# Three of four panels of a norm turned in 32x32 blocks on VectorE and moved by DMA, and the last GLA head ordered right behind its values

## The chip, the cores and the metric

The kernel is one launch on one core of a Trainium2 chip. Its time is device time in microseconds (us), and runs of the two kernels are compared on the same chip. The engines are TensorE (PE; the loading of its weights is shown as PEld), VectorE (DVE), ScalarE (ACT), GpSimd (POOL) and SyncE (SP), which here only issues transfers.

## The reference

A decoder trunk of two layers works on one sequence of 256 tokens by 2048 features, with 256 memory tokens. All is float32.

```
for i in range(DEPTH):                        # DEPTH = 2
    if i == 1:
        fk, fv, fc = fox_shared_kv(x, ...)    # rmsnorm(x) @ w_kv, forget gates
    h = rmsnorm(x, norm_mix[i])
    x = x + (gla_mixer if i == 0 else fox_mixer)(h, ...)
    h = rmsnorm(x, norm_ffn[i])
    x = x + conv_ffn(h, ...)                  # 2048 -> 2 x 5632 -> 2048
return rmsnorm(x, norm_final)
```

The first layer mixes with chunked gated linear attention (GLA, 4 heads), the second with forgetting attention (FoX, 12 heads). Both also attend to the memory tokens with 4 more heads, and the output projection takes all of these side by side. The GLA mixer scales each head's output by a norm of its own and multiplies it with a gate, silu(og). A projection contracts over features, so it wants h with features on the partitions; x itself is kept with tokens on the partitions. Between the two x has to be turned.

## The kernel before

**Products.** Every weight is cut into a high part that PE takes in a single pass and a low remainder. `split_unit` (line 189) loads a unit of 128x1024 floats (512 KB) into one of four `raw` buffers (line 200), ScalarE makes `whi` (205) and VectorE `wlo` (206), each with four buffers. Activations are kept as two halves too: `split` (302) lets ScalarE write the high half times the norm's gain (309) and VectorE the remainder (310). A projection with features out, `proj_fm` (209), runs 32 products of 128x512 on the high parts (line 230) and 32 of 128x256 on the low parts (228). A projection with tokens out, `proj_tm` (242), takes per unit 8 products on `whi` and 4 on `wlo` (line 271), for two token blocks of 128.

**Order.** The body is one program text, and a scheduler with a model of the machine puts it in order on each engine before it runs. `high_priority(offset=AHEAD)` draws weight loads and casts forward, and `issue_after` keeps an instruction behind a named one. Each engine then works strictly in its order, and so does SP's queue of transfers, on which all weight loads stand.

**Where x is turned.** `add_out` (862) runs a projection in four panels of 512 features; its `evac` adds a panel to x (865) and calls `then(f, b)` for token block b. `preparing(name, dst, also)` (903) makes that `then`: it adds squares for the norm's sums (393), and once both token blocks of a panel are there it turns the panel: 8 transpositions of 128x128 on PE into PSUM bank `ps_s` (916), and four `split` calls from PSUM into `dst` (918). It is used three times: behind the first output projection for `ffn0`, behind the down projection of the first feed-forward for the FoX keys and values (`kv`), and behind the second output projection for `ffn1`. At `kv` two norms with different gains need the same x: `also` (930) copies the first 12 turned chunks from PSUM into the buffer `vt` (932), which is not yet in use, and `fox` (757) splits them from there for its queries (`stash`, lines 759 and 769). The final norm keeps tokens on partitions and turns nothing.

**Around the last GLA head.** `gla` (532) runs through the heads: gates (579), query, key and value projections, then `core` (602), which prepares decayed copies of queries and keys on VectorE and ScalarE and makes the scores in small products on PE (651, 658, 667, 673: the half tiles between chunks, the levels inside a chunk, and the rest). `core(hd, ..., ahead)` has `issue_after(ends[-1])`, the last product of the value projection, and `issue_after(ahead)`; `ahead` is the product that spreads the norm of the head before (`made[1].spread`, line 377), except for head 0. `outputs` (696) multiplies scores with values (703, 704), and `scale` (712) applies the head's norm, made by `mean` (334) and `row` (375 to 380). Six gate projections `take_og` (717) follow, two of them before the last head's values; the last head's `outputs` is called at `j == OG_EARLY + 1` and its `scale` at `j == OG_EARLY + 2`. The first output projection takes the memory heads' chunks first, then those of the GLA heads in order.

Of the kernel before, what the change touches and what calls it, by code (L numbers as in the profile page):

```python
# [12 lines left out]
F32 = mybir.dt.float32  # L13
F32R = mybir.dt.float32r
I32 = mybir.dt.int32
AF = mybir.ActivationFunctionType
ALU = mybir.AluOpType
PSUM = bass.MemoryType.PSUM

P = 128  # L20
T = 256
# [4 lines left out]
GLA_H, DK, DV = 4, 256, 384  # L26
# [14 lines left out]
OG_EARLY = 2  # L41
# [99 lines left out]
def _trunk(ctx: ExitStack, tc: tile.TileContext, xt, xtok, memt, wp, wgu, gns, gfin, cnv, par, msk, out):  # L141
    nc = tc.nc
    where, _ = _layout()
    V, S, TE = nc.vector, nc.scalar, nc.tensor
# [8 lines left out]
    part = const.tile([P, C_N], F32, name="part")  # L153
# [6 lines left out]
    def gain(name, i):  # L160
        c = C_GAIN[name] + i
        return gains[:, c : c + 1]
# [6 lines left out]
    x = [const.tile([P, 2, 512], F32, name=f"x{f}") for f in range(4)]  # L169
    bufA = [const.tile([P, 2, T], F32R, name=f"A{i}", tag=f"A{i}") for i in range(KC)]  # L170
# [11 lines left out]
    loads, casts, ends = [], [], []  # L182
# [119 lines left out]
    def split(dst, i, src, g=None):  # L302

        hi, lo = dst[i][:, 0, :], dst[i][:, 1, :]
        if g is None:
            S.activation(hi, src, AF.Copy)  # L306
            V.tensor_tensor(lo, src, hi.bitcast(F32), ALU.subtract)
        else:
            S.activation(hi, src, AF.Copy, scale=g)
            V.scalar_tensor_tensor(lo, src, g, hi.bitcast(F32), ALU.mult, ALU.subtract)  # L310

    class Norm:

# [142 lines left out]
    nx = StreamNorm()  # L456
# [75 lines left out]
    def gla(nx):  # L532
        h, mix = bufB, bufA
        with tc.tile_pool(name="gla", bufs=1) as gp:
# [161 lines left out]
            def outputs(hd, v):  # L696
                at = att[hd % 2]
                nrm = Norm(DV, "o" if hd < GLA_H - 1 else "m")
                os = []
                for j in range(3):  # L700
                    po = work("o")
                    vs = slice(j * P, (j + 1) * P)
                    TE.matmul(po[:, :T], v[:, 0, vs], at[:, :T], start=True, stop=False)  # L703
                    TE.matmul(po[:, P:T], v[:, 1, vs], at[:, T:], start=False, stop=True)  # L704
                    o = gp.tile([P, T], F32, name="onorm", tag="onorm", bufs=9)
                    on[3 * hd + j] = o
                    S.activation(o, po[:, :T], AF.Copy)
                    nrm.add(o)
                    os.append(o)
                return hd, nrm, os  # L710

            def scale(hd, nrm, os):
                for j, o in enumerate(os):
                    f = C_GN + 3 * hd + j
                    V.scalar_tensor_tensor(o, o, part[:, f : f + 1], nrm.row(), ALU.mult, ALU.mult)
# [13 lines left out]
            for hd in range(GLA_H):  # L729
                bc = gates(hd)  # L730
                q = gp.tile([P, 2, T], F32, name="gq", tag="gq", bufs=2)
                k = gp.tile([P, 2, T], F32, name="gk", tag="gk", bufs=2)
                v = values(hd) if hd else v0
                proj_fm(("gq", hd), h, lambda c, a: V.scalar_tensor_tensor(
                    q[:, c, :], whole(a), DK ** -0.5, nx.row(), ALU.mult, ALU.mult))
                if hd:
                    made = outputs(hd - 1, vs)
                proj_fm(("gk", hd), h, lambda c, a: V.tensor_tensor(k[:, c, :], whole(a), nx.row(), ALU.mult))
                if hd:
                    scale(*made)  # L740
                if hd == GLA_H - 1:
                    for j in range(OG_EARLY):
                        take_og(j)
                if hd:
                    proj_tm(("gv", hd), h, lambda b, a: S.activation(
                        v[:, b, :], a, AF.Copy, scale=nx.col()[:, b : b + 1]))
                core(hd, q, k, bc, made[1].spread if hd else ends[-1])
                vs = v
            for j in range(OG_EARLY, 6):
                if j == OG_EARLY + 1:  # L750
                    made = outputs(hd, vs)
                if j == OG_EARLY + 2:
                    scale(*made)
                take_og(j)


    def fox(nx, vt):
        hk, hq, mix = bufB, bufA, bufB
        stash = vt.rearrange("p b (i t) -> p (b i) t", t=T)
        with (  # L760
            tc.tile_pool(name="fox", bufs=1) as fp,
            tc.tile_pool(name="foxd", bufs=1, space=bass.MemoryType.DRAM) as dp,
# [3 lines left out]
            for j in range(6):  # L766
                proj_fm(("fk", j), hk, lambda c, a, j=j: V.tensor_tensor(kt[:, 2 * j + c, :], whole(a), nx.row(), ALU.mult))
                for i in range(2 * j, 2 * j + 2):
                    split(hq, i, stash[:, i, :], gain("mix1", i))
            cs = fp.tile([P, T], F32, name="fc")  # L770
            cc = fp.tile([P, 2, FOX_H], F32, name="fcc")
            take, turn = turned(fp, work("s", 2), FOX_H, nx.col())
# [89 lines left out]
    def add_out(key, src, then=None, spare=None, last=None):  # L862
        for f in range(4):
            def evac(b, a, f=f):
                V.tensor_tensor(x[f][:, b, :], x[f][:, b, :], a, ALU.add)
                if then is not None:
                    then(f, b)

            proj_tm((*key, f), src, last if f == 3 and last is not None else evac, spare if f == 3 else None)

    def ffn(l, nx, h, m, then, spare=None, last=None):
        with tc.tile_pool(name=f"ffn{l}", bufs=1) as fp:
            cw = fp.tile([P, 4 * 88], F32, name="cw")
            nc.sync.dma_start(cw, cnv[l])
            us = [fp.tile([P, T + 2], F32, name=f"u{i}") for i in range(4)]
            for u in us:
                nc.gpsimd.memset(u[:, :2], 0.0)
            turn = [0]
            for p, (lo, hi) in enumerate(PARTS):
                for j in range(lo, hi):  # L880
                    cv = {}

                    def evac(c, a, j=j, cv=cv, i=j - lo):
                        u = us[turn[0] % 4]
                        turn[0] += 1
                        V.tensor_tensor(u[:, 2:], whole(a), nx.row(), ALU.mult)  # L886
                        col = (c * 44 + j) * 4
                        w = [cw[:, col + n : col + n + 1] for n in range(4)]
                        r = fp.tile([P, T], F32, name=f"cv{c}", tag=f"cv{c}", bufs=3)
                        S.activation(r, u[:, 2:], AF.Identity, bias=w[3], scale=w[2])  # L890
                        V.scalar_tensor_tensor(r, u[:, 1 : T + 1], w[1], r, ALU.mult, ALU.add)
                        V.scalar_tensor_tensor(r, u[:, :T], w[0], r, ALU.mult, ALU.add)
                        cv[c] = r
                        if c == 1:
                            S.activation(cv[0], cv[0], AF.Silu)
                            V.tensor_tensor(r, cv[0], r, ALU.mult)  # L896
                            split(m, i, r)

                    proj_fm(("up", l, j), h, evac)
                end = p == len(PARTS) - 1  # L900
                add_out(("down", l, p), m, then if end else None, spare if end else None, last if end else None)

    def preparing(name, dst, also=None):
        n = StreamNorm()

        def then(f, b):
            n.add(f, b)
            if b == 0:
                return
            for i in range(4 * f, 4 * f + 4, 2):  # L910
                ps = work("s", 2)
                for j in range(2):
                    for c in range(2):
                        o = j * T + c * P
                        k = (i + j) % 4 * P
                        TE.transpose(ps[:, o : o + P], x[f][:, c, k : k + P], ident)  # L916
                for j in range(2):
                    split(dst, i + j, ps[:, j * T : (j + 1) * T], gain(name, i + j))
                if also is not None:
                    also(i, ps)  # L920

        return n, then

    gla(nx)
    n, then = preparing("ffn0", bufB)
    add_out(("wo", 0), bufA, then)
    with tc.tile_pool(name="stash", bufs=1) as st:
        vt = st.tile([P, 2, FOX_H * HD], F32, name="fvt")

        def also(i, ps):  # L930
            if i < 12:
                S.activation(vt.rearrange("p b t -> p (b t)")[:, i * T : (i + 2) * T], ps, AF.Copy)
            else:
                for j in range(2):
                    split(bufA, i + j, ps[:, j * T : (j + 1) * T], gain("mix1", i + j))

        n2, then = preparing("kv", bufB, also)
        ffn(0, n, bufB, bufA, then)
        fox(n2, vt)
    n, then = preparing("ffn1", bufA)  # L940
    add_out(("wo", 1), bufB, then)


    fin = StreamNorm()
# [115 lines left out]
```

## Time and profile before

| | |
|---|---|
| three runs | 2284.09 to 2286.19 us, median 2285.31 |
| the profiled execution | 2284.91 us, span 2282.9 |
| PE, DVE, ACT busy | 2269.7, 1588.6, 1259.0 us |
| weights loaded by SP's queue | 809 transfers, most of 512 KB |
| L916, transpositions of x on PE | 96 |

The profile shows one execution. A row of a timeline is start, length, engine, line, operation, output<-inputs, shape and count of merged instructions. A group has busy time and the mean length of one instruction in ns. PE's instructions overlap, so lengths and busy times of small ones are more than the time they take up; starts tell that. What is idle on an engine costs nothing unless it lies on the chain that ends last.

### The profile page before, as it was taken

To read this page: it belongs to the slowest core of one execution; us is meant where nothing else is said; L and a number is where in the kernel's file an instruction comes from. 1 tells how busy PE (TensorE), PEld (TensorE's weight loads), DVE (VectorE), ACT (ScalarE), POOL (GpSimd) and SP (SyncE) were. 2 spreads that over 40 slices of the span, in tenths; PEclk is the share of its full clock that TensorE was granted. 3 is DMA by queue.
4 is the path that set the end of the run, shared out by engine and by line. 5 is a ranking of instruction groups with operands and counts; after the bars stand their busy time and mean duration, and the time that the engine had idled before them with its cause. 6 is when DMAs were issued, how large, how long until landed. Compare 5 with 4: busy or idle time off the path is not lost.

```text
span 2282.9 us, 33393 instructions
## 1 busy us (share of the span) xinstructions
PE 2269.7 (99%) x12417; PEld 1985.8 (87%) x12417; DVE 1588.6 (70%) x2618; ACT 1259.0 (55%) x2001; POOL 3.4 (0%) x19
## 2 busy tenths in 40 slices
PE   9999999999999999999999999999999999999998
PEld 8889998788888888888888998888888888888887
DVE  7769786677765777557766567657776577756775
ACT  6656576555553555445565555556554455534554
POOL 0000000000000000000000000000000000000000
PEclk9999999999999999999999999999999999999999
DMA  9655555555566555655555665555666566665664
GB/s 342 195 164 168 177 171 168 165 183 190 190 194 193 185 192 190 199 186 191 190 187 179 183 195 166 174 191 178 194 189 198 186 190 187 194 194 185 193 194 147
DMA packets 125610, 430.19 MB, mean 188 GB/s; under 512 B 14204, under 2 KB 19464, under 8 KB 125320
## 3 DMA queue, kind: packets, MB, share of 16 engines
q1 hardware_dynamic: 124872, 427.27, 58.0%
q8 instruction: 97, 1.59, 0.3%
q10 hardware_dynamic: 576, 0.79, 0.1%
q14 instruction: 65, 0.53, 0.1%
HBM read 425.90 MB, written 2.11 MB: 187 GB/s over the span
## 4 chain that ended last, share of the span: by engine, by line
PE 99%; DVE 0%; ACT 0%; issue 0%; DVEq 0%; ACTq 0%
PE acc L230 39%; PE acc L271 37%; PE acc L228 20%; PE ps_s L916 0%; PE ps_s L658 0%; PE ps_t L409 0%; PE ps_o L430 0%; PE ps_s L430 0%; PE ps_s L828 0%; PE ps_o L844 0%; PE ps_o L703 0%; PE ps_o L180 0%; PE ps_o L845 0%; PE ps_s L827 0%; PE ps_o L704 0%; PE ps_t L377 0%
## 5 line engine op out<-in xcount | busy, mean ns | idle before, releaser
L206 DVE TENSOR_TENSOR wlo<-raw,whi 128x1024 fp32r<-128x1024 f32 (+4 forms) x809 | 969.1, 1201 | 562.6 <-ACT whi L205 463.6
L205 ACT ACTIVATE whi<-raw 128x1024 fp32r<-128x1024 f32 (+4 forms) x809 | 840.2, 1039 | 607.4 <-PE acc L271 324.3
L230 PE MATMUL acc<-B,whi 128*128 128x512 f32 x2112 | 496.5, 390 | 0.0
L230 PEld LDWEIGHTS acc<-B,whi 128*128 128x128 f32 x2112 | 391.1, 188 | 77.6
L271 PE MATMUL acc<-whi,mix 128*128 128x512 f32 x1280 | 321.8, 391 | 2.6 <-ACT mix L306 2.6
L230 PE MATMUL acc<-mix,whi 128*128 128x512 f32 x1248 | 303.5, 391 | 0.0
L271 PEld LDWEIGHTS acc<-whi,mix 128*128 128x128 f32 x1280 | 240.3, 188 | 52.7 <-ACT mix L306 2.8
L228 PEld LDWEIGHTS acc<-B,wlo 128*128 128x128 f32 x2112 | 264.6, 191 | 5.7
L230 PEld LDWEIGHTS acc<-mix,whi 128*128 128x128 f32 x1248 | 230.2, 188 | 45.2
L228 PE MATMUL acc<-B,wlo 128*128 128x256 f32 x2112 | 269.4, 283 | 0.0
L271 PE MATMUL acc<-whi,B 128*128 128x512 f32 (+3 forms) x960 | 218.1, 363 | 0.0
L271 PEld LDWEIGHTS acc<-whi,B 128*128 128x128 f32 x960 | 174.5, 188 | 17.8
L271 PE MATMUL acc<-wlo,mix 128*128 128x512 f32 x640 | 175.9, 392 | 0.0
L228 PEld LDWEIGHTS acc<-mix,wlo 128*128 128x128 f32 x1248 | 157.8, 191 | 4.3
L228 PE MATMUL acc<-mix,wlo 128*128 128x256 f32 x1248 | 161.3, 284 | 0.0
L271 PEld LDWEIGHTS acc<-wlo,mix 128*128 128x128 f32 x640 | 120.1, 189 | 24.7
L230 PE MATMUL acc<-A,whi 128*128 128x512 f32 x544 | 133.7, 390 | 0.0
L237 ACT ACTIVATE part<-acc 128x256 f32<-128x256 f32 x244 | 92.4, 379 | 61.4 <-PE acc L230 61.3
L271 PE MATMUL acc<-wlo,B 128*128 128x512 f32 (+3 forms) x480 | 120.8, 363 | 0.0
L230 PEld LDWEIGHTS acc<-A,whi 128*128 128x128 f32 x544 | 101.6, 188 | 20.7
L306 ACT ACTIVATE mix<-cv 128x256 fp32r<-128x256 f32 x60 | 25.1, 418 | 161.3 <-DVE cv L896 161.3
L890 ACT ACTIVATE cv<-u,cw 128x256 f32<-128x256 f32 x176 | 104.9, 596 | 8.7 <-DVE u L886 8.6
(230 smaller groups left out, 1674.7 us busy)
## 6 DMA issues: line engine op xcount, KB each, us to landing
raw<-wp SPq DMA_DIRECT2D x743, 512.0 KB, 3.7
raw<-wp SPq DMA_DIRECT2D x32, 384.0 KB, 3.4
raw<-wp SPq DMA_DIRECT2D x24, 388.0 KB, 3.5
raw<-wp SPq DMA_DIRECT2D x8, 400.0 KB, 3.3
xf<-xt SPq DMA_DIRECT2D x16, 128.0 KB, 5.5
x<-xtok SPq DMA_DIRECT2D x4, 512.0 KB, 9.0
mt<-memt SPq DMA_DIRECT2D x7, 256.0 KB, 6.5
cb<-cdram SPq DMA_DIRECT2D x12, 128.0 KB, 3.1
```

Of the source, the lines that this page charges most:

```text
L205: casts.append(S.activation(hi[:, s], raw[:, s], AF.Copy))
L206: V.tensor_tensor(lo[:, s], raw[:, s], hi[:, s].bitcast(F32), ALU.subtract)
L228: TE.matmul(acc[c][:, :T], w[:, s], both[:, 0, :], start=False, stop=False)
L230: TE.matmul(acc[c], w[:, s], both, start=u == j == 0, stop=(u, j) == (3, 3))
L237: S.activation(t, a[:, T:], AF.Copy)
L271: mm = TE.matmul(acc[b][:, :n], src[kcs[j] - base][:, part, b * P : (b + 1) * P], w, start=u == 0 and low == part == j == 0, stop=u == end ...
L306: S.activation(hi, src, AF.Copy)
L890: S.activation(r, u[:, 2:], AF.Identity, bias=w[3], scale=w[2])
```

## The change

For panels 0 to 2 of the three turned norms, PE no longer turns x. VectorE turns each 128x512 token block in 32x32 blocks into a buffer `blk`; when both token blocks are done, 16 transfers of 32 partitions by 1 KB put the blocks on their partitions in a second buffer, and `split_turned` makes the halves from there: one pass of 128x256 on ScalarE and two of 128x128 on VectorE for each chunk. Panel 3 stays on PE. At `kv` the second buffer is the `vt` area itself, so the copies from PSUM are gone, and `fox` splits from that area with `split_turned`.

In `gla` the last head's `core` is no longer held behind the spread of the head before, only behind its own value projection (`ends[-1]`), and its `scale` is called together with its `outputs`, one gate earlier.

```diff
+    def split_turned(dst, i, z, name):
+        g = gain(name, i)
+        hi, lo = (dst[i][:, part, :].rearrange("p (b q j) -> p b q j", b=2, q=4) for part in range(2))
+        src = z[:, :, i % 4].rearrange("p q b j -> p b q j")
+        S.activation(hi, src, AF.Copy, scale=g)
+        for b in range(2):
+            V.scalar_tensor_tensor(lo[:, b], src[:, b], g, hi[:, b].bitcast(F32), ALU.mult, ALU.subtract)
...
-                core(hd, q, k, bc, made[1].spread if hd else ends[-1])
+                core(hd, q, k, bc, made[1].spread if 0 < hd < GLA_H - 1 else ends[-1])
...
                 if j == OG_EARLY + 1:
-                    made = outputs(hd, vs)
-                if j == OG_EARLY + 2:
-                    scale(*made)
+                    scale(*outputs(hd, vs))
...
                 for i in range(2 * j, 2 * j + 2):
-                    split(hq, i, stash[:, i, :], gain("mix1", i))
+                    split_turned(hq, i, stash[i // 4], "mix1")
...
+        def turned_panel(f, b):
+            if b == 0:
+                blocks[f] = pool.tile([P, 4, 4, 2, 32], F32, name="blk", tag="blk", bufs=2)
+            y = blocks[f]
+            V.transpose(y[:, :, :, b, :], x[f][:, b, :].rearrange("p (k c i) -> p c k i", c=4, i=32))
+            if b == 0:
+                return
+            z = pool.tile([P, 4, 4, 2, 32], F32, name="turn", tag="turn", bufs=2) if kept is None else kept[f]
+            for q in range(4):
+                for c in range(4):
+                    nc.sync.dma_start(z[32 * c : 32 * (c + 1), q], y[32 * q : 32 * (q + 1), c])
+            for k in range(4):
+                split_turned(dst, 4 * f + k, z, name)
...
         def then(f, b):
             n.add(f, b)
+            if f < 3:
+                turned_panel(f, b)
+                return
             if b == 0:
                 return
...
         def also(i, ps):
-            if i < 12:
-                S.activation(vt.rearrange("p b t -> p (b t)")[:, i * T : (i + 2) * T], ps, AF.Copy)
-            else:
-                for j in range(2):
-                    split(bufA, i + j, ps[:, j * T : (j + 1) * T], gain("mix1", i + j))
+            for j in range(2):
+                split(bufA, i + j, ps[:, j * T : (j + 1) * T], gain("mix1", i + j))
```

More of the change, by code (lines that the diff above doesn't have):

```diff
@@ L750, in gla, with fox @@
                 if j == OG_EARLY + 1:
-                    made = outputs(hd, vs)
-                if j == OG_EARLY + 2:
-                    scale(*made)
+                    scale(*outputs(hd, vs))
                 take_og(j)
-    def fox(nx, vt):
+    def fox(nx, vt, stash):
         hk, hq, mix = bufB, bufA, bufB
-        stash = vt.rearrange("p b (i t) -> p (b i) t", t=T)
         with (
@@ L901, in ffn, with preparing @@
                 add_out(("down", l, p), m, then if end else None, spare if end else None, last if end else None)
-    def preparing(name, dst, also=None):
+    def preparing(name, dst, pool, kept=None, also=None):
         n = StreamNorm()
+        blocks = {}
+        def turned_panel(f, b):
[11 more added lines that the diff above has]
+                split_turned(dst, 4 * f + k, z, name)
         def then(f, b):
             n.add(f, b)
+            if f < 3:
+                turned_panel(f, b)
+                return
             if b == 0:
@@ L924, in _trunk @@
     gla(nx)
-    n, then = preparing("ffn0", bufB)
-    add_out(("wo", 0), bufA, then)
+    with tc.tile_pool(name="turn0", bufs=1) as tp:
+        n, then = preparing("ffn0", bufB, tp)
+        add_out(("wo", 0), bufA, then)
     with tc.tile_pool(name="stash", bufs=1) as st:
         vt = st.tile([P, 2, FOX_H * HD], F32, name="fvt")
+        turned3 = vt.rearrange("p b t -> p (b t)").rearrange("p (f q k b j) -> p f q k b j", f=3, q=4, k=4, b=2)
+        turned3 = [turned3[:, f] for f in range(3)]
         def also(i, ps):
-            if i < 12:
-                S.activation(vt.rearrange("p b t -> p (b t)")[:, i * T : (i + 2) * T], ps, AF.Copy)
-            else:
-                for j in range(2):
-                    split(bufA, i + j, ps[:, j * T : (j + 1) * T], gain("mix1", i + j))
[L937 to L941, printed above, removed]
+            for j in range(2):
+                split(bufA, i + j, ps[:, j * T : (j + 1) * T], gain("mix1", i + j))
+        with tc.tile_pool(name="turn1", bufs=1) as tp:
+            n2, then = preparing("kv", bufB, tp, turned3, also)
+            ffn(0, n, bufB, bufA, then)
+        fox(n2, vt, turned3)
+    with tc.tile_pool(name="turn2", bufs=1) as tp:
+        n, then = preparing("ffn1", bufA, tp)
+        add_out(("wo", 1), bufB, then)
     fin = StreamNorm()
```

## The prediction

> **What bounds the kernel now.** The page is read first: its span, part 1 (engines) and part 4 (the chain of work that ended last).
>
> ```profile
> span 2282.9 us, 33393 instructions
> PE 2269.7 (99%) x12417; PEld 1985.8 (87%) x12417; DVE 1588.6 (70%) x2618; ACT 1259.0 (55%) x2001; POOL 3.4 (0%) x19
> ...
> PE 99%; DVE 0%; ACT 0%; issue 0%; DVEq 0%; ACTq 0%
> ```
>
> TensorE is busy for 99% of the span and is 99% of the chain. A busy PE need not be a full one, so the waits of PE come next, and then the windows of the two later stages that the change touches and of one short stretch (columns: the stretch, its length, busy time and count of each engine, granted clock, DMA share, GB/s).
>
> ```profile
> PE acc L271 <- ACT mix L306: 2.6, 1, 2.6
> PE ps_o L180 <- DVE B L177: 1.4, 1, 1.4
> PE ps_t L377 <- DVE dg L375: 1.1, 1, 1.1
> ```
>
> ```profile
> 1137.00:1205.00 68.00, 68.00 (x314) 56.31 (x313) 46.48 (x64) 43.78 (x85) 0.31 (x1) 1.00 0.60 193
> ...
> 1472.00:1560.00 88.00, 88.00 (x423) 73.73 (x422) 52.01 (x76) 45.47 (x80) 0.20 (x4) 1.00 0.58 193
> ```
>
> ```profile
> 413.40:417.50 4.10, 4.04 (x11) 3.19 (x12) 1.18 (x4) 1.68 (x4) 0.20 (x4) 0.58 0.17 46
> ```
>
> PE waits three times in all. L180 is the start and stays. The other two lie together, in the first output projection, and the stretch behind them ran at a granted clock of 0.58. The stages at 1137 and 1472 us, where x is also turned, have no gap on PE at all. So time can come from two things only: less work on PE, and that one stall. DVE has 21.5 us free in 68.
>
> **Part 1: 72 of the 96 transpositions on PE go** (three panels of four, three norms, eight each). The group, then the timeline of PE about one panel:
>
> ```profile
> L916 PE MATMUL ps_s<-mask,x 128*128 128x128 f32 x96 | 14.3, 272 | 0.0
> ```
>
> ```profile
> 1151.17 1.98 PE L271 MATMUL acc<-whi,mix 128*128 128x512 f32 x8
> 1152.99 1.07 PE L271 MATMUL acc<-wlo,mix 128*128 128x512 f32 x4
> 1153.89 1.53 PE L271 MATMUL acc<-whi,mix 128*128 128x512 f32 x6
> 1155.26 0.38 PE L916 MATMUL ps_s<-mask,x 128*128 128x128 f32 x2
> 1155.39 0.71 PE L271 MATMUL acc<-whi,mix 128*128 128x512 f32 x2
> 1155.94 0.39 PE L271 MATMUL acc<-wlo,mix 128*128 128x512 f32 x1
> 1156.17 0.82 PE L916 MATMUL ps_s<-mask,x 128*128 128x128 f32 x6
> 1156.74 0.94 PE L271 MATMUL acc<-wlo,mix 128*128 128x512 f32 x3
> 1157.52 1.98 PE L271 MATMUL acc<-whi,mix 128*128 128x512 f32 x8
> ```
>
> Durations overlap, so slots are read from starts. Twelve products from 1151.17 to 1153.89: 2.72 us, 0.227 each; that is also one weight unit (8 high, 4 low). From 1153.89 to 1157.52, 3.63 us, lie again twelve products and 8 transpositions: (3.63 - 2.72) / 8 = 0.114 us each. 72 x 0.114 = **8.2 us**. The group's busy time gives 14.3 / 96 = 0.149 and 10.7 us, which I keep as an end of the range.
>
> A sentence apart: the Trainium skill, page "TensorE: Matmul & The Clock Gate", section "Part 4: PE-mode transpose", gives about 275 ns for one transposition inside a kernel; an estimate by that page would be 72 x 0.275 = 19.8 us.
>
> **Part 2: the last GLA head moves forward.** PE's timeline at the stall (the brackets are idle time and its cause):
>
> ```profile
> 408.05 1.07 PE L271 MATMUL acc<-whi,mix 128*128 128x512 f32 x4
> 410.21 0.63 PE L377 MATMUL ps_t<-dg,onesr 128*128 128x256 f32 x2 [1.09 <-DVE dg L375]
> 413.46 2.68 PE L271 MATMUL acc<-whi,mix 128*128 128x512 f32 x6 [2.63 <-ACT mix L306]
> 415.94 1.66 PE L271 MATMUL acc<-wlo,mix 128*128 128x512 f32 x4
> 417.44 1.09 PE L271 MATMUL acc<-whi,mix 128*128 128x512 f32 x4
> ```
>
> The four products at 408.05 give their slots up at 408.96. Until 413.46 only the two L377 run, so 4.2 us are lost (3.9 to 4.5, as the two take 0.63 or almost nothing). The ten products up to 417.44 take 3.98 us for 2.27: 1.7 us more, at the clock of 0.58. Together **5.9 us**. The cause is a late chain: the head's norm row (L334 to L377), then gate and split. Its start was held back:
>
> ```profile
> 321.30 3.83 PE L230 MATMUL acc<-B,whi 128*128 128x512 f32 x16
> ...
> 368.23 1.98 PE L271 MATMUL acc<-whi,A 128*128 128x512 f32 x8
> ```
>
> ```profile
> 332.22 2.18 DVE L644 TENSOR_TENSOR gdd<-gdd,gq 128x384 f32<-128x384 f32 x6
> ...
> 371.19 0.61 PE L651 MATMUL ps_s<-gq,gk 128*128 128x128 f32 x4
> ...
> 402.13 0.61 PE L334 MATMUL ps_t<-mask,ssq 128*128 128x128 f32 x4
> ```
>
> VectorE had the operands ready at 334.4, but PE began the head's scores at 371.19, since they were ordered behind the norm of the head before. The four gate projections behind the value projection run from 321.30 to 368.23; without what is interleaved one is 32 products of 0.227 and 32 half ones of 0.12, 11.1 us. In the built order of the changed kernel the scores stand two gates and twelve products in, 321.3 + 22.2 + 2.7 = 346.2, and the head's outputs and norm follow in the last gate. From the norm's L334 to its L377 stand 55 products of 0.227, 12.5 us, where the chain now needs 410.2 - 402.1 = 8.1; from L377 to the first product that needs the result stand 29, 6.6 us, where it now needs 413.5 - 410.2 = 3.3. Both are covered, so the stall goes. What is late next is the norm of the head before: between its L334 and L377 stand 19 products, 21 half ones and two pairs of the last head's, some 8.0 us, and ScalarE has one more table switch in between, as a Silu stands between logarithm and exponential. I put 0.5 us there (0 to 2).
>
> **Part 3: what replaces the transpositions.** Per panel: 2 block turns on DVE, 16 transfers of 32 KB on SP's queue, and splits from SBUF. Prices by the nearest rows:
>
> ```profile
> L206 DVE TENSOR_TENSOR wlo<-raw,whi 128x1024 fp32r<-128x1024 f32 x743 | 906.3, 1223 | 505.8 <-ACT whi L205 409.5 <-issue 59.1 <-PE acc L228 30.8
> L205 ACT ACTIVATE whi<-raw 128x1024 fp32r<-128x1024 f32 x743 | 784.6, 1056 | 557.1 <-PE acc L271 290.0 <-PE acc L230 163.9 <-ACT whi L205 52.6
> ...
> L865 DVE TENSOR_TENSOR x<-x,acc 128x512 f32<-128x512 f32 x62 | 42.4, 686 | 17.8 <-PE acc L271 17.4
> ...
> L310 DVE SCALAR_TENSOR_TENSOR B<-ps_s,gains,B 128x256 fp32r<-128x256 f32 x32 | 14.7, 478 | 9.4 <-ACT B L309 9.4
> ...
> L309 ACT ACTIVATE mix<-fvt,gains 128x256 fp32r<-128x256 f32 x12 | 5.4, 497 | 0.0
> ...
> L822 DVE SCALAR_TENSOR_TENSOR dm<-cb,fcc,mask 128x128 f32<-128x128 f32 x12 | 4.1, 340 | 0.0
> ```
>
> No row shows a block turn. Between a 128x128 pass (0.34) and a 128x1024 pass (1.22) I take the row of its size, 0.69. DVE: 18 x 0.69 = 12.3 us, and 96 low halves of 0.34 for 48 of 0.478, 9.7 us more: 22 us over nine panels, 2.4 us each, beside 5 us or more of free DVE per panel (21.5 us over the four panels from 1137). ScalarE keeps its 48 high halves at about 0.5 us and loses six copies. Neither engine is on the chain, so this costs nothing; were DVE full, PE would wait for the low halves of weights, 2.4 us a panel.
>
> Transfers (KB each, median us from issue to landing; then SP's own time to issue one, min/median/max ns):
>
> ```profile
> raw<-wp SPq DMA_DIRECT2D x743, 512.0 KB, 3.7
> ...
> xf<-xt SPq DMA_DIRECT2D x16, 128.0 KB, 5.5
> x<-xtok SPq DMA_DIRECT2D x4, 512.0 KB, 9.0
> ...
> out<-x SPq DMA_DIRECT2D x4, 128.0 KB, 2.2
> ```
>
> ```profile
> L200 SPq DMA_DIRECT2D raw<-wp x809: 327/328/680, 0.7 to 2254.6; - x162
> ```
>
> The program lets eight transfers be in flight on SP's queue, each waiting for the one eight ahead. So one takes the larger of its issue, 0.33, and landing / 8: 0.28 to 0.69 for landings of 2.2 to 5.5. I take 3.7 / 8 = 0.46. A panel of the down projection lasts 6 units = 16.3 us and needs 16 + 6 transfers: 10.1 us. An output projection has 8 units = 21.8 us and 16 + 8 transfers: 11.0 us. SP keeps up.
>
> New waits: SP waits for the block turn, with weight loads queued behind it; ScalarE and VectorE wait for all 16 transfers, with weight casts queued behind. Cover: four weight buffers, so a cast may begin when PE leaves a unit and PE needs it three units, 8.2 us, later; less its own 1.06 that is 7.1 us. A load is issued about 10.9 us ahead of its cast and lands in 3.7: some 5 us more. The built order puts a panel's splits two casts behind the unit whose landing frees its last transfers, which is just about when these land. The third panel is needed after the next stage's first 7 us and has 1 to 4 us to spare. I cost all this at nothing; without that cover it is what the rival below costs.
>
> **The sum**, against the profiled execution (span 2282.9, whole time 2284.9): 2284.9 - 8.2 - 5.9 + 0.5 = 2271.3. The shown runs have a median of 2285.3, 0.4 above it; I leave the forecast at **2271.3 us**.
>
> **Rivals.**
> - *Small waits take back part*: splits or casts come 0.5 to 1 us late at each of nine panels. For it: the third panel's margin of 1 to 4 us. Against: the 12 us of cover. Price 4.5 to 9 us, **2278**.
> - *The last head stalls elsewhere*, the 5.9 us staying: **2277**. For it: the head before has 8.0 us for a chain with one more table switch. Against: 12.5 and 6.6 us of cover for the last head.
> - *SP's queue becomes the bound* (the slower side). If a turned transfer holds it for t, a down panel needs 16 t + 6 x 0.33 us of 16.3; it keeps up until t = 0.9, a landing of 7 us. Past it each panel slips, and after the 12 us of cover PE waits. At t = 2.2 (transfers one at a time, landing as the stores) a down panel slips by 21 us and an output panel by 16: (3 x 21 - 12) + 2 x (3 x 16 - 12) = 123 us, **2394**. It ends slower than before from about t = 1.4 (22.4 + 2 - 16.3 = 8.1, three times, less 12 = 12; the output panels 22.4 + 2.6 - 21.8 = 3.2 add nothing). For it: x landed in 9.0 us. Against: that was 512 KB beside the first weight loads.
> - *A transposition holds PE for its own 272 ns*: 72 x 0.272 = 19.6 us, **2259.9**. Against: the starts at 1156.17 and 1156.74, six in 0.57 us. This is where the page named above would land.
>
> The rule that speaks against the change stands apart: the Trainium skill, page "DMA: Bandwidth & Descriptors", section "Bandwidth", says that transfers under 64 KB are dominated by descriptors; no run shown here has such a transfer between partitions, and an estimate by its fixed cost of about 2 us would put one at 2.1 us alone, or 0.26 with eight in flight.
>
> **Numbers.** Forecast 0.60; small waits 0.17; stall elsewhere 0.10; SP's queue 0.10; longer transpositions 0.03. The low end takes the busy-time price: 2271.3 - 2.5, rounded to **2268.5**. The high end takes both middle rivals' prices short of their sum, **2281**. Outside remain SP's queue, the long transpositions and a tail of the middle rivals, some 0.2. A change under 0.2% (4.6 us) is about what cannot be told from none: faster is below 2280.7, slower above 2289.9. Faster 0.81, same 0.09 (tails of the middle rivals, and a weak form of SP's), slower 0.10.
>
> **What would show it.** In the new trace: 24 transpositions; PE without a wait in the first output projection and no stretch at a clock of 0.58; scores of the last head near 346 us; block turns near 0.7 us; turned transfers landing within 4 us; no ScalarE or DVE wait on them over about 5 us; PE gapless at the starts of the up and key projections. Any of the last three missed, with PE gaps behind it, makes the forecast wrong; so does a new wait at L377's successor for the third head.

## The result and the profile after

| | before | after |
|---|---|---|
| median (range) | 2285.07 us (2284.09 to 2286.19, 4 runs) | 2272.56 us (2272.54 to 2272.87, 4 runs) |
| span of the profiled execution | 2282.9 us | 2270.7 us |

The ratio is 0.9946, with a 95% interval of 0.9934 to 0.9958: 12.5 us less. The forecast was 2271.3 us, 13.6 us below the profiled execution of before (2284.9). The page of the changed kernel, span, engines and chain of work:

```profile
span 2270.7 us, 33489 instructions
...
PE 2259.8 (100%) x12345; PEld 1977.1 (87%) x12345; DVE 1603.6 (71%) x2684; ACT 1256.6 (55%) x1996; POOL 3.4 (0%) x19
...
PE 99%; ACT 0%; DMA 0%; issue 0%; DVE 0%; SPq 0%; DVEq 0%
```

PE still sets the time. It has 72 instructions fewer and is busy 9.9 us less. VectorE took on 15.0 us and ScalarE lost 2.4; neither shows in the chain. The waits of PE (total, times, longest, in us), and the window that held the slow stretch before:

```profile
PE ps_o L180 <- DVE B L177: 1.4, 1, 1.4
PE ps_o L712 <- ACT onorm L716: 1.0, 1, 1.0
PE acc L271 <- ACT whi L205: 0.5, 1, 0.5
```

```profile
413.40:417.50 4.10, 4.10 (x20) 3.40 (x19) 1.77 (x2) 1.50 (x2) 0.00 (x0) 1.00 0.82 240
```

Both waits of the first output projection are gone, and in the same 4.1 us PE does 20 instructions at a clock of 1.00 instead of 11 at 0.58. There is one new wait, at L712, an output pair of the last head; the 0.5 us belong to the first unit of the program, at 9 us, and not to the change. The new operations, as groups and as DMA issues (the last number is median us to landing), then SP's own time to issue one (ns, min/median/max):

```profile
L921 DVE STREAM_TRANSPOSE blk<-x 128x512 f32<-128x512 f32 x18 | 12.7, 707 | 0.3
...
L319 DVE SCALAR_TENSOR_TENSOR B<-turn,gains,B 128x128 fp32r<-128x128 f32 x24 | 6.7, 346 | 3.6 <-ACT B L317 3.6
...
L317 ACT ACTIVATE B<-turn,gains 128x256 fp32r<-128x256 f32 x12 | 5.1, 498 | 5.7 <-DMA turn<-blk 5.7
...
L944 PE MATMUL ps_s<-mask,x 128*128 128x128 f32 x24 | 3.6, 272 | 0.0
```

```profile
turn<-blk SPq DMA_DIRECT2D x96, 32.0 KB, 3.6
...
fvt<-blk SPq DMA_DIRECT2D x48, 32.0 KB, 3.3
```

```profile
L927 SPq DMA_DIRECT2D turn<-blk x96: 507/588/1520, 408.1 to 1526.7; - x96
L927 SPq DMA_DIRECT2D fvt<-blk x48: 507/588/1335, 1147.4 to 1191.4; - x48
```

Block turns (0.707 us), low halves (0.346), high halves (0.498) and landings (3.6 and 3.3) are near the forecast's 0.69, 0.34, 0.5 and 3.7. The issue is not: 0.588 us where a weight load's 0.33 had been taken.

### The profile page after: what moved, and what is told of

It is laid out like the page before. It is cut to its first block, busy times and chain, and to the rows that moved or that the text cites. A ratio compares the mean times of both kernels' runs of the same rounds, so it can differ in the third digit from the quotient of the medians.

```text
span 2270.7 us, 33489 instructions
## 1 busy us (share of the span) xinstructions
PE 2259.8 (100%) x12345; PEld 1977.1 (87%) x12345; DVE 1603.6 (71%) x2684; ACT 1256.6 (55%) x1996; POOL 3.4 (0%) x19
## 4 chain that ended last, share of the span: by engine, by line
PE 99%; ACT 0%; DMA 0%; issue 0%; DVE 0%; SPq 0%; DVEq 0%
PE acc L230 39%; PE acc L271 37%; PE acc L228 20%; PE ps_s L667 0%; PE ps_t L418 0%; DMA raw<-wp 0%; PE ps_o L439 0%; PE ps_s L439 0%; PE ps_s L834 0%; PE ps_o L850 0%; PE ps_o L712 0%; ACT whi L205 0%; PE ps_s L833 0%; PE ps_o L851 0%; PE ps_s L944 0%
```

## The experiments

Three theories of where 12.5 us came from, and why it was less than the 13.6 forecast. **A**: the transpositions pay their PE slots in full, and the last head pays its stall less something that comes back in its own region. **B**: the head pays in full, and the panels give something back to small waits. **C**: the head pays nearly everything, and the transpositions were hidden beside other work. "Below before" is always against runs of the kernel before on the same chip (medians 2285.33, 2285.51, 2285.54 and 2285.09 in the four groups of runs).

### Each half of the change alone

The last head alone, on the kernel before:

```diff
-                core(hd, q, k, bc, made[1].spread if hd else ends[-1])
+                core(hd, q, k, bc, made[1].spread if 0 < hd < GLA_H - 1 else ends[-1])
...
-                    made = outputs(hd, vs)
-                if j == OG_EARLY + 2:
-                    scale(*made)
+                    scale(*outputs(hd, vs))
```

> The kernel before with the last head's edit alone (scores not held behind the head before, scale called with the outputs); all 96 transpositions stay on PE. Theory A (the panels pay their PE slots, 0.114 us each, and the head pays the stall of 5.9 us less about 2 us that come back: a 1.0 us wait of PE on ScalarE at the third head's last output pair, and about 0.9 us more for score products mixed with output pairs): about -3.9 us, 2281.2. Theory B (the head pays the whole forecast of 5.4 us, and the panels give some back to small waits): about 2279.7. Theory C (the head pays nearly all and the transpositions hide beside other work): about -12, 2273.

Measured: 2280.91 us, 4.4 below before, ratio 0.9981 (0.9972 to 0.9990).

The three panels alone; the diff is the same one turned round, on the changed kernel:

> The changed kernel with the last head as before: three panels of four go over VectorE and transfers, the stall in the first output projection stays. Theory A: 72 x 0.114 = 8.2 us less than before, 2276.9, and the stall's two waits (about 1.1 and 2.6 us) and the stretch at a lowered clock are there again. Theory B: about 7 us less, 2278. Theory C: about 2284.

Measured: 2277.39 us, 7.9 below before, ratio 0.9965 (0.9953 to 0.9977). The two halves make 12.3 of the 12.5 us, so they add up and C falls: the head alone does not give 12 us. The start of the second feed-forward's first up projection on PE shows it without the scatter between runs, in the kernel before, with the head alone, and in the changed kernel:

```profile
1544.96 1.29 PE L230 MATMUL acc<-mix,whi 128*128 128x512 f32 x5
```

```profile
1541.19 3.79 PE L230 MATMUL acc<-mix,whi 128*128 128x512 f32 x16
```

```profile
1532.87 3.79 PE L230 MATMUL acc<-mix,whi 128*128 128x512 f32 x16
```

The head gives 3.77 us, the 72 transpositions another 8.32: 0.116 us each. In the run with the panels alone the stall is there again, and so is the slow clock (last row: the window of before, now at 0.50):

```profile
413.61 2.93 PE L271 MATMUL acc<-whi,mix 128*128 128x512 f32 x6 [2.63 <-ACT mix L306]
416.33 1.91 PE L271 MATMUL acc<-wlo,mix 128*128 128x512 f32 x4
418.04 1.75 PE L271 MATMUL acc<-whi,mix 128*128 128x512 f32 x4
419.63 1.09 PE L271 MATMUL acc<-wlo,mix 128*128 128x512 f32 x4
...
413.40:417.50 4.10, 3.90 (x9) 3.12 (x10) 1.32 (x4) 1.70 (x4) 0.20 (x4) 0.50 0.16 46
```

The wait is the 2.63 us of before to the hundredth, but 14 products behind it, from 413.61 to 419.63, are slow here, and take 6.02 us for 14 x 0.227 = 3.18; before it was 10. The price of one and the same gap so varied by 1.1 us. The Trainium skill, page "TensorE: Matmul & The Clock Gate", section "Why this matters for your kernels", warns of PE gaps over about 3 us because the clock drops behind them; here gaps of 1.09 and 2.63 us, with only two short products between, were enough.

### How many panels

```diff
-            if f < 3:
+            if f < 2:
```

(and for chunks 8 to 11 at `kv` the copies and splits of the kernel before)

> The changed kernel with two panels of four turned by VectorE and transfers and two on PE (48 transpositions on PE instead of 24). Theory A: 24 x 0.114 = 2.7 us slower than the changed kernel, 2275.3, whatever the third panel's late transfers do. Theory B (the third panel, the one with 1 to 4 us to spare, gives back part of its gain): under 2 us slower, 2274.5 or less. If a transposition held PE for its whole 0.272 us: 6.5 us slower, 2279.

Measured: 2275.27 us, ratio 0.9956 (0.9943 to 0.9968), 10.1 below before. Seen from the head alone, 48 transpositions fewer give 5.6 us, 0.118 each, and the last 24 another 2.4 to 2.7, 0.10 to 0.11. The third panel gives back next to nothing, so B falls too. Its margin can be read in the changed kernel at `kv`, first on ScalarE, then on PE:

```profile
1195.80 1.71 ACT L317 ACTIVATE B<-fvt,gains 128x256 fp32r<-128x256 f32 x4 [1.11 <-DMA fvt<-blk]
```

```profile
1193.48 3.79 PE L230 MATMUL acc<-B,whi 128*128 128x512 f32 x16
1197.11 0.52 PE L228 MATMUL acc<-B,wlo 128*128 128x256 f32 x3
...
1197.59 0.48 PE L228 MATMUL acc<-B,wlo 128*128 128x256 f32 x2
...
1198.49 2.52 PE L228 MATMUL acc<-B,wlo 128*128 128x256 f32 x19
```

Eight chunks take 32 products: 16 on the high parts and 16 on the low. The third panel's first low product is the twelfth of the 19 from 1198.49, at about 1199.8, and its last chunk follows 0.7 us later; the four high halves are done at 1197.5, some 3 us ahead.

All four panels, the other way:

```diff
-            if f < 3:
+            if f < 4:
...
-            z = pool.tile([P, 4, 4, 2, 32], F32, name="turn", tag="turn", bufs=2) if kept is None else kept[f]
+            z = pool.tile([P, 4, 4, 2, 32], F32, name="turn", tag="turn", bufs=2) if kept is None or f == 3 else kept[f]
...
                 split_turned(dst, 4 * f + k, z, name)
+                if also is not None and f == 3:
+                    split_turned(bufA, 4 * f + k, z, "mix1")
```

> The changed kernel with all four panels turned by VectorE and transfers, none on PE. Slots alone would give 2.7 us less, 2269.9. Theory A adds the chain of the last panel: from its sums on, a block turn of 0.7 us, 16 transfers at the 0.63 us that SP took for each, with weight loads between them (about 13.4 us), a landing of 3.3 and splits of 2 make about 19 us, while the next stage has 8.3 us of products that do not need it, 16.6 if the first two column blocks are mixed: a stall of 3 to 11 us after each norm, 2277 to 2300. A rival says that this chain is hidden as the others are: 2270.

Measured: 2297.96 us, ratio 1.0056 (1.0042 to 1.0070): 12.6 above before. Its waits of PE:

```profile
PE acc L228 <- ACT B L317: 8.4, 2, 5.2
PE acc L228 <- ACT A L317: 7.0, 1, 7.0
PE ps_t L386 <- DVE dg L384: 3.9, 3, 2.5
```

Three norms wait 19.3 us together, 6.4 each, and PE is busy 4.3 us longer than in the changed kernel (2264.1 us) although 24 transpositions of 0.114 are gone: 7.0 us that go with a lower granted clock (0.994 over the execution, against 0.999). 19.3 + 4.3 = 23.6, and the span grew by 23.8. So the panel that ends a stage is worth its place on PE.

### SP's queue

The slower rival of the prediction, by cutting each transfer in two and in four, with the same bytes:

```diff
-                    nc.sync.dma_start(z[32 * c : 32 * (c + 1), q], y[32 * q : 32 * (q + 1), c])
+                    for h in range(2):
+                        nc.sync.dma_start(z[32 * c + 16 * h : 32 * c + 16 * (h + 1), q],
+                                          y[32 * q + 16 * h : 32 * q + 16 * (h + 1), c])
```

> The changed kernel with each transfer of 32 partitions cut into two of 16 partitions, 32 of 16 KB per panel instead of 16 of 32 KB, the same bytes. If the 0.59 us that SP took to issue one goes with its rows, two halves take as long as one whole, and the time stays at 2272.6. If it is fixed for each transfer, a down panel needs 32 x 0.63 + 6 x 0.55 = 23.5 us of SP's queue where PE has 16.3, an output panel 24.6 of 21.8: by the slower rival's sum, (3 x 7.2 - 12) + 0 = 10 us, about 2282; the third panel's late splits at the next stage come on top.

> The same, cut into four transfers of 8 partitions: 64 of 8 KB per panel. If issue goes with the rows: 2272.6. If it is fixed: a down panel needs 64 x 0.63 + 3.3 = 43.6 us of SP's queue for 16.3, an output panel 44.7 for 21.8; (3 x 27.3 - 12) + 2 x (3 x 22.9 - 12) = 183 us, about 2455, with PE waiting for casts of weights, as the slower rival says.

Measured: 2321.72 us in halves, ratio 1.0158 (1.0142 to 1.0173), and 2517.34 us in quarters, ratio 1.1014 (1.0994 to 1.1034). Issue in the two:

```profile
L928 SPq DMA_DIRECT2D turn<-blk x192: 507/587/1393, 408.4 to 1588.0; - x192
```

```profile
L928 SPq DMA_DIRECT2D turn<-blk x384: 624/624/1267, 408.1 to 1784.3; - x192
```

SP needs 0.59 us to issue a transfer of 32 rows, 0.59 for 16 and 0.62 for 8: it is a price per transfer. The expectation had that, but 10 us for the halves where 49 came (2321.72 against 2272.56), and 183 for the quarters where 245 came. The waits of PE say where:

```profile
PE acc L228 <- ACT B L317: 16.7, 2, 10.2
PE ps_t L386 <- DVE dg L384: 9.8, 2, 5.2
PE acc L228 <- ACT mix L317: 6.2, 1, 6.2
PE acc L230 <- DVE nt L352: 4.0, 1, 4.0
```

They make 36.7 us, and PE is busy 11.6 us more for the same work, at a lowered clock; the span grew by 48.5. The window of the longest wait, where the clock is 0.78:

```profile
1212.00:1250.00 38.00, 24.02 (x118) 21.32 (x119) 22.42 (x67) 17.10 (x33) 0.31 (x1) 0.78 0.41 141
```

No wait lies in an output or down projection, so nothing came of the 10 us that the expectation put there. All of them lie at the start of the next stage. 22.9 us (L317) are for the third panel's high halves, which that stage wants some 6 us in. The rows of the other 13.8 name the norm's own chain on VectorE (L352, L384), but the transfers stand behind these too. The first row below is of PE at `kv`, the others are of ScalarE and VectorE behind the first output projection:

```profile
1215.73 3.75 PE L230 MATMUL acc<-B,whi 128*128 128x512 f32 x8 [4.02 <-DVE nt L352]
```

```profile
479.20 1.06 ACT L205 ACTIVATE whi<-raw 128x1024 fp32r<-128x1024 f32 x1 [3.21 <-DMA raw<-wp]
480.29 1.23 DVE L206 TENSOR_TENSOR wlo<-raw,whi 128x1024 fp32r<-128x1024 f32 x1 [1.40 <-ACT whi L205]
481.50 0.75 DVE L384 TENSOR_TENSOR dg<-mask,y 128x256 fp32r<-128x256 f32 x2
```

The product at 1215.73 reads B and not nt: it waited for the second panel, whose high halves ScalarE began only at 1214.31. In the 9.8 us on L384, ScalarE stood idle 3.2 us (3.6 at the third norm) for a weight load that was queued behind the transfers, and the norm's `dg` stands on VectorE behind that unit's remainder. In quarters the casts are late inside the panels as well:

```profile
PE acc L271 <- ACT whi L205: 66.3, 10, 20.0
PE acc L228 <- ACT B L317: 64.7, 2, 36.0
```

The same queue from the other side: four panels, every second transfer on GpSimd's queue.

```diff
-                    nc.sync.dma_start(z[32 * c : 32 * (c + 1), q], y[32 * q : 32 * (q + 1), c])
+                    (nc.gpsimd if c % 2 else nc.sync).dma_start(z[32 * c : 32 * (c + 1), q],
+                                                                y[32 * q : 32 * (q + 1), c])
```

> All four panels by VectorE and transfers, as in the run with four, but every second transfer issued on GpSimd's queue instead of SP's. With four panels on SP's queue alone PE waited about 19 us for the last panel's halves and spreads, three norms together. Theory A (SP's queue, 0.59 us to issue each of 16 and the weight loads between, is the long part of that chain): a queue with half of them needs 6.7 us instead of 13.4, the stall falls by about 6 us per norm, to 2270 to 2283. Rival (GpSimd issues no faster than 1.2 us each, or the landing and splits are the long part): 2290 to 2300.

Measured: 2279.86 us, ratio 0.9975 (0.9966 to 0.9984). GpSimd issues in 0.496 us, and 18 of the 25 us go:

```profile
PE acc L228 <- ACT B L317: 2.9, 2, 2.6
PE ps_t L386 <- DVE dg L384: 2.5, 1, 2.5
PE ps_o L180 <- DVE B L177: 1.5, 1, 1.5
PE ps_o L712 <- ACT onorm L716: 1.0, 1, 1.0
PE acc L228 <- ACT A L317: 0.7, 1, 0.7
```

SP's issue was the long part of the last panel's chain; 6.1 us of waits are left for 2.7 us of slots, and PE is busy 2.5 us longer than in the changed kernel, so four panels still lose to three.

### What the last head gives back

ScalarE in the changed kernel, ahead of the new wait (PE resumed at 367.92):

```profile
362.86 1.28 ACT L363 ACT_TABLE_LOAD   x1
364.15 0.20 ACT L363 ACTIVATE ny<-nv 128x2 f32<-128x2 f32 x1
364.37 1.28 ACT L732 ACT_TABLE_LOAD   x1
365.67 0.42 ACT L732 ACTIVATE gate<-gate 128x256 f32<-128x256 f32 x1
366.10 1.28 ACT L364 ACT_TABLE_LOAD   x1
367.39 0.20 ACT L364 ACTIVATE ny<-ny 128x2 f32<-128x2 f32 x1
367.50 0.37 ACT L716 ACTIVATE onorm<-ps_o 128x256 f32<-128x256 f32 x1
```

Logarithm, Silu and exponential each load a table, 3.84 us in all, and the copy that frees the output bank for the next pair (L716) stands behind them. Two ways out were tried. No tables for this head's norm:

```diff
-                nrm = Norm(DV, "o" if hd < GLA_H - 1 else "m")
+                nrm = Norm(DV, "o" if hd < GLA_H - 2 else "m")
```

> The changed kernel with the third head's norm made by Newton steps on VectorE alone, as the last head's is, so that no logarithm and exponential tables are loaded on ScalarE there. Theory A (PE's wait of 0.98 us on the onorm copy comes from four table loads of 1.28 us that stand ahead of that copy): the wait goes, about 2271.6. Rival: the wait comes from the order of ScalarE's work and stays, 2272.6. Newton's chain on VectorE is longer, so the spread of this norm comes later and the order of the last output pairs moves with it.

Measured: 2272.09 us, ratio 0.9940 (0.9928 to 0.9953). The wait is gone from the profiled execution, which was the fastest of five (2270.75 us, span 2269.0); the median lies halfway between the two expectations and decides nothing. Or the scores behind the third output pair of the head before:

```diff
+                    pairs.append(TE.matmul(po[:, P:T], v[:, 1, vs], at[:, T:], start=False, stop=True))
...
-                core(hd, q, k, bc, made[1].spread if 0 < hd < GLA_H - 1 else ends[-1])
+                core(hd, q, k, bc, (made[1].spread if hd < GLA_H - 1 else pairs[-1]) if hd else ends[-1])
```

> The changed kernel with the last head's scores held behind the third output pair of the head before, so that score products and output pairs no longer alternate on PE. Theory A (alternating shapes cost about 0.9 us: 5.37 us for the scores and two pairs where the scores alone took 3.37 before and two pairs among the gate products 1.14): about 2271.7, if the later scores stay covered (7 us later, of 12.5 us of cover less 8.1). Rival: the 0.9 us is not the mixing, or the wait on ScalarE moves along: 2272.6 to 2274.

Measured: 2270.75 us, ratio 0.9935 (0.9923 to 0.9948), span 2268.8; 1.0 us below the 2271.7 expected. ScalarE then has logarithm and exponential side by side, and this wait is gone here too. Both together:

> The changed kernel with both repairs of the last head's region at once: scores behind the third output pair of the head before, and that head's norm by Newton steps on VectorE. Each alone removed the wait of 0.98 us on ScalarE; the first gave 1.8 us, the second 0.5. Theory A (the wait can only go once, and the mixing of score products and output pairs is the rest): the same as the first alone, 2270.7. Rival (the two gains are separate): 2270.2 or less. If Newton's longer chain comes too late behind the later scores: above 2271.5, with a wait of PE at the spread.

Measured: 2271.62 us, ratio 0.9939 (0.9926 to 0.9953), span 2269.8: no more than the second alone, and above the 2271.5 of the last expectation, but without its wait at the spread. Its profiled execution waits 0.6 us for a weight cast at 1200 us, where the stage behind the second norm's panels begins. A gain of under 2 us is near what a run can tell, so the changed kernel and this version were timed side by side:

> The changed kernel itself once more, timed beside the next run on the same chip, so that the two can be set against each other and not only against the kernel before: 2272.6, with PE's wait of about 1.0 us on the onorm copy and the first up projection starting on PE about 142.7 us after the first gate projection behind the values.

> The version with the last head's scores held behind the third output pair, on the same chip as the changed kernel. If what it takes out is there in every execution: 1.8 to 2.2 us below the changed kernel, 2270.6, without the wait, and about 140.9 us between the two starts. Rival: the earlier 2 us were scatter between chips, and the two agree within 0.5 us.

Measured: 2272.27 us (2272.09 to 2273.26) against 2270.71 (2270.58 to 2271.87), five runs each, with spans of 2270.6 and 2268.9. The first up projection starts at 464.08 and 462.24 us:

```profile
464.08 3.79 PE L230 MATMUL acc<-B,whi 128*128 128x512 f32 x16
```

```profile
462.24 3.79 PE L230 MATMUL acc<-B,whi 128*128 128x512 f32 x16
```

So the scores behind the pairs are worth 1.6 to 1.8 us, 1.0 of it the wait. The remaining 0.6 to 0.8 was expected of alternating shapes (0.9), which is not shown. In the profiled execution with Newton steps scores and pairs alternate as before (5.37 us), and yet the first up projection starts 141.2 us after the first gate projection behind the values, where it is 142.7 in the changed kernel and 140.9 with the scores behind the pairs. So in that execution most of the gain is there without an end to the alternation; what the rest of the order does stays open.

## Why the prediction was right, step by step

- **Part 1, the slots: right.** 0.114 us from starts was forecast; 0.116 (72 in the starts at the second up projection) and 0.118 (48, by medians) were measured, 8.3 us for 8.2. The busy-time price of 0.149 and the rival's 0.272 fall. The Trainium skill, page "TensorE: Matmul & The Clock Gate", section "Part 4: PE-mode transpose", which the prediction named, gives about 275 ns for one transposition; the group of after does show 272 ns for one, but that is its own length, overlapped with its neighbours, and what goes away with it is its slot.
- **Part 2, the last head: mechanism right, gain too large.** The scores began at 346.27 us (forecast 346.2), the stall and the slow stretch vanished. The net was 3.8 us by PE's starts (4.4 by medians) where 5.4 stood in the sum, so 2.1 us of the 5.9 came back where the prediction had put 0.5 (range 0 to 2) for "one more table switch". The loads cost a wait of 1.0 us, at another place than forecast: the prediction looked at the third head's norm row (L377's successor), which had no wait; it fell on the copy behind the loads, and so on the next output pair. The order that it named, a Silu between logarithm and exponential, was the cause: without the two tables (Newton steps) the wait is gone, and so it is where they stand side by side (scores behind the pairs). For the other 1.1 us the prediction has no term. 0.6 to 0.8 of them went with the scores behind the pairs; their cause stays open. The rival that has the last head stall elsewhere was right in kind, at 2.1 us and not 5.9.
- **Part 3, the replacement: hidden, as forecast**, but with less room on SP than written. Issue is 0.588 us, and of four in a row (2.41 us with the last one's 0.51) one follows the other in 0.63, where 0.46 was forecast from landing / 8. A down panel so needs 16 x 0.63 + 6 x 0.55 = 13.4 us of 16.3 instead of 10.1. VectorE took 15 us more, not 22. The third panel's halves came some 3 us ahead of need, inside the 1 to 4 forecast. Landings were not all within the 4 us that the prediction asked for: some took up to 5.9, with no gap on PE behind them.
- **The rival of SP's queue: right in kind, wrong in its threshold.** It was to end slower than before from 1.4 us per turned transfer. Two halves at 0.63 make 1.26 us, and that was already 36 us slower than before. The formula counted only weight casts late inside a stage, and in halves there was none. What failed lies at the start of the next stage: the third panel, needed some 6 us into it, then the second panel and a weight load behind the transfers, and the granted clock was down to 0.78 in the longest of these stretches.
- **The sum**: what the forecast missed, 1.3 us, is the head's term: 1.6 us, less 0.1 more from the slots. With what was measured the sum reads 2284.9 - 8.3 - 3.8 = 2272.8, against the median of 2272.56.

The Trainium skill, page "DMA: Bandwidth & Descriptors", section "Bandwidth", which spoke against the change, has transfers under 64 KB dominated by descriptors. Landing, of whole transfers and then of halves, agrees in part, as its median fell by less than a third for half the bytes:

```profile
DMA to landing us min/median/max: 1.8/3.5/5.9
```

```profile
DMA to landing us min/median/max: 1.7/2.5/8.4
```

But what made small transfers dear here was the issuing engine's time for each, which the runs in halves and quarters show.

## What to carry to other kernels

Price a small instruction on a full pipelined engine by the starts of its neighbours with and without it, not by its length or busy time. When work moves to a transfer queue, count its issues, each at its own measured price, and look for the first consumer with a deadline: here the first products of the next stage, not the weights of the stage in which the transfers run. When an edit mixes two chains on ScalarE, count the table loads that now stand ahead of a copy that frees a bank.

## What the runs showed of the hardware

- SP took 0.588 us to issue a transfer between partitions, whether of 32 or 16 rows of 1 KB, and 0.624 for 8 rows, against 0.328 for a 128-row weight load (0.53 for one between turned transfers); GpSimd took 0.496.
- VectorE turned 128x512 floats in 32x32 blocks in 0.707 us, near the time of an addition of that size (0.686).
- The same PE gap of 2.63 us was followed by 10 slow products in one kernel and 14 in another, 1.7 and 2.8 us.
